# Projections of a hybrid decoder's front: three passes of rounded halves, or pairs of 64-column f32 matmuls

## The chip, the cores and the metric

The kernel runs on one core of one Trainium2 chip. The metric is device time in microseconds (us); lower is better. TensorE (PE) does the matmuls, VectorE (DVE), ScalarE (ACT) and GpSimd (POOL) the rest; SyncE's queue (SP) issues most loads.

## The reference, cut to what matters

One layer of a decoder: an input projection, three branches (dilated attention, a conformer convolution, cross-attention into 256 memory tokens), gates on their projections, an output projection, and a mixture of 32 experts of which each token takes two. 512 prompt rows and 32 sample rows go through it, all in f32.

```python
z_q, z_k, z_v, z_conv, z_mq, z_gate = split_combined(h @ lw['w_in'])
...
kv = rms_norm(mem, lw['mem_norm_g']) @ lw['w_mem_kv']
...
z = jax.nn.sigmoid(g_a) * a + jax.nn.sigmoid(g_c) * c + jax.nn.sigmoid(g_m) * m
return z @ w_out
...
for e in range(N_EXPERTS):
    hid = jax.nn.silu(h @ lw['w_expert_gate'][e]) * (h @ lw['w_expert_up'][e])
    y = y + gates[:, e:e + 1] * (hid @ lw['w_expert_down'][e])
```

## The kernel before

The front, to about 700 us, is everything ahead of the experts. Its projections go through two helpers. `mm_nat` multiplies a block of 128 rows by 256 columns of weights, with the activations stationary: the memory keys and values (`mem_kv`, 64 blocks of 128 x 128 x 256), the four heads (`project_head`, 384) and the output projection (128), 576 in all. `mm_T` keeps the weights stationary and streams half of the 544 rows (272): the gated units of the convolution (`glu`, 128 blocks), the gates (384) and the branch projections (192) of `branch`, 704 in all.

For each block both helpers issue three f32r matmuls of 128 stationary columns: high half by high half, and the two cross terms, added up in PSUM. The halves are made by `split`: ACT rounds a block of weights to f32r (`hi`, L230) and DVE subtracts it from the original (`lo`, L231). The normed rows `hTh`/`hTl`, the memory rows, the branches' inputs (`split_src`), their weights (`split_p`) and the sum ahead of the output projection (`zh`/`zl`) are kept as halves in the same way. A weight block is loaded into a slot of `ring` (six slots of 8 KB per partition, given out in turn) and its slot comes free when the halves are made; the halves stand in pool `whl` (two `hi`, two `lo`).

Between the projections PE does attention and other small work: transposes and scores of 128 columns, and matmuls of 32 columns such as `sample` (L402) and the router's logits (L1216), which put several narrow matmuls into different column ranges of the array. The experts (from 707 us) already use f32 pairs: `pg` and `pu` at L1535 (64 stationary columns, 256 streamed), `pd` at L1555 (64 and 512).

The scheduler writes each engine's order; each engine then runs its list in order and waits on semaphores. SP issues its loads in order too, so a load that waits for its slot holds back what stands behind it. Expert weights start to load when blocks come free near the end of the front.

Of the kernel before, what the change touches and what calls it, by code (L numbers as in the profile page):

```python
# [12 lines left out]
F32R = mybir.dt.float32r  # L13
# [8 lines left out]
P = 128  # L22
# [130 lines left out]
def build(tc, I, O, cols):  # L153
# [68 lines left out]
    last_lo = [None]  # L222

    def split(t, eng=(nc.vector,), pl=None):
        hi = (pl or whl).tile([P, 8, 256], F32R, name=nm("hi"), tag="w" if pl else "hi")
        lo = whl.tile([P, 8, 256], F32R, name=nm("lo"), tag="lo")
        n = 8 // len(eng)
        for q, e in enumerate(eng):
            s = slice(q * n, q * n + n)
            nc.scalar.copy(hi[:, s], v8(t)[:, s])  # L230
            last_lo[0] = e.tensor_tensor(lo[:, s], v8(t)[:, s], hi[:, s].bitcast(F32), op=ALU.subtract)  # L231
        return hi, lo
# [20 lines left out]
    hTh = hp.tile([P, 8, NT], F32R, name="hTh")  # L253
    hTl = hp.tile([P, 8, NT], F32R, name="hTl")

# [8 lines left out]
    def t_tile(name):  # L264
        return tp.tile([P, 5 * NP], F32R, name=name, tag="T")

# [11 lines left out]

    memhl = mhl.tile([P, 2, 8, NMEM], F32R, name="memhl")
    memh, meml = memhl[:, 0], memhl[:, 1]  # L280
# [3 lines left out]
    hTs = hs_.tile([P, 8, NS], F32, name="hTs", bufs=1)  # L284
# [12 lines left out]
    def loadx(src, key, at, alloc=None):  # L297
        n = src.shape[0]
        if key not in xt:
            xt[key] = alloc(nm("x")) if alloc else t_tile(nm("x")).bitcast(F32)  # L300
        v = xt[key][:, at * D:(at + 1) * D]
        last_load[0] = nc.sync.dma_start(v[:n], src)
        return v
# [33 lines left out]
    def rms_T(x, n, g, hi, lo, off, fs=None):  # L337
# [5 lines left out]
        for half in range(2):  # L343
            ps = tr.tile([P, 4, P], F32, name=nm("tr"), tag="tr")
            for kk in range(4):
                k = half * 4 + kk
                nc.tensor.transpose(ps[:, kk, :n], x[:n, k * P:(k + 1) * P], ident[:n, :n])
            c = slice(half * 4, half * 4 + 4)
            hs = hi[:, c, off:off + n]
            nc.scalar.copy(hs, ps[:, :, :n])  # L350
            nc.vector.tensor_tensor(lo[:, c, off:off + n], ps[:, :, :n], hs.bitcast(F32), op=ALU.subtract)
            if fs is not None:
                nc.scalar.copy(fs[:, c, :], ps[:, :, :n])

    for i in range(2):
        rms_T(xm[i], P, "mem_norm_g", memh, meml, i * P)
# [63 lines left out]
    def project_head(h, units, extra=()):  # L420
        T = t_tile(nm("T")).bitcast(F32).rearrange("p (s t) -> p s t", s=5)
        vh = hd.tile([P, 4, HD], F32, name=nm("vh"), tag="vh")
        vp = hd.tile([P, 4, HD], F32, name=nm("vp"), tag="vp")
        for u in range(3):
            wh, wl = split(units[u], H0ENG if h == 0 else (nc.vector,))
            for p in extra[3 + u:4 + u]:
                p.load()
            for ip in range(2):
# [3 lines left out]
                for i2 in range(2):  # L432
                    i = 2 * ip + i2
                    s = slice(i * P, (i + 1) * P)
                    mm_nat(ps[:, i2], [hTh[:, k, s] for k in range(8)], [hTl[:, k, s] for k in range(8)],
                           [wh[:, k, :] for k in range(8)], [wl[:, k, :] for k in range(8)])
# [119 lines left out]
    H0ENG = (nc.vector,) * 2  # L556
    MENG = (nc.vector, nc.vector, nc.vector, nc.gpsimd)
    def mem_kv(us_):
        al = slice(None)
        for u in us_:  # L560
            wh, wl = split(munits[u], MENG)
            ps = mm.tile([P, 2, 2, HD], F32, name=nm("mm"), tag="mm")
            for i2 in range(2):
                s = slice(i2 * P, (i2 + 1) * P)
                mm_nat(ps[:, i2], [memh[:, k, s] for k in range(8)], [meml[:, k, s] for k in range(8)],
                       [wh[:, k, :] for k in range(8)], [wl[:, k, :] for k in range(8)])
# [28 lines left out]
    class Scores:  # L595
# [3 lines left out]
        def load(self):  # L599
            h, j = self.h, self.j  # L600
            t = raw()
# [24 lines left out]
    rms_T(xs[0], P, "norm_mix_g", hTh, hTl, 0 * P)  # L626
    rms_T(xs[1], P, "norm_mix_g", hTh, hTl, 1 * P)
    mem_kv([0])
    rms_T(xs[2], P, "norm_mix_g", hTh, hTl, 2 * P)
    mem_kv([1])  # L630
    rms_T(xs[3], P, "norm_mix_g", hTh, hTl, 3 * P)
    rms_T(xs[4], NS, "norm_mix_g", hTh, hTl, NP, hTs)
# [18 lines left out]
    for h in range(4):  # L651
# [9 lines left out]
        if h == 3:  # L661
            uraw = t_tile("u").bitcast(F32)
            u = uraw[:, :4 * (30 + NP)].rearrange("p (c t) -> p c t", c=4)
            cw = uraw[:, 4 * (30 + NP):4 * (30 + NP) + 136].rearrange("p (c t) -> p c t", c=4)
            cTf = t_tile("cT").bitcast(F32)[:, :4 * NT].rearrange("p (c t) -> p c t", c=4)
# [35 lines left out]
    def mm_T(ps, wh, wl, xh, xl):  # L701
        n = len(wh)
# [5 lines left out]
    def halves(t, n):  # L708
        return [[t[:, k, f * HALF:(f + 1) * HALF] for k in range(n)] for f in range(2)]

    hH, hL = halves(hTh, 8), halves(hTl, 8)
# [30 lines left out]
    def glu(c, unit, st_tile, pl=None):  # L742
        hi, lo = split(unit, pl=pl)
        if c >= NGH:
            taps(TG[0], last_lo[0])
        half = lambda t, a: [t[:, k, a * P:(a + 1) * P] for k in range(8)]
        for f in range(2):
            pa = mm.tile([P, HALF], F32, name=nm("mm"), tag="mm")
            pb = mm.tile([P, HALF], F32, name=nm("mm"), tag="mm")
            mm_T(pb, half(hi, 1), half(lo, 1), hH[f], hL[f])  # L750
            mm_T(pa, half(hi, 0), half(lo, 0), hH[f], hL[f])
# [17 lines left out]

    for c in range(NGH):  # L770
# [4 lines left out]
    for p in pieces:  # L775
# [32 lines left out]
    def branch_loads(br, wname, j):  # L808
        gu = split(load_cols(w_in, [(GCOL + br * D + j * P, 256)]))
# [142 lines left out]
    glu(3, c3, kt_tile, ring)  # L952
# [24 lines left out]
    for f in range(NPG):  # L977
        pgs.append(mm.tile([P, HALF], F32, name=nm("mm"), tag="mm"))
        mm_T(pgs[f], *([t[:, k, :P] for k in range(8)] for t in pre[0]), hH[f], hL[f])
# [6 lines left out]
    zh, zl = [], []  # L986
    zs = zp.tile([P, 8, NS], F32, name="zs")
# [3 lines left out]
    pl_ = mst.enter_context(pool("pw", 2, side="right"))  # L991

    shs = [mg.tile([P, 4, NT], F32R, name=nm("sh"), tag="sh", bufs=2) for _ in range(2)]

    def split_src(src, lo):
        sh = shs.pop(0) if shs else mg.tile([P, 4, NT], F32R, name=nm("sh"), tag="sh", bufs=2)
        out = []
        for c in range(4):
            nc.scalar.copy(sh[:, c], src[c])
            out.append(lo(c))  # L1000
            nc.vector.tensor_tensor(out[c], src[c], sh[:, c].bitcast(F32), op=ALU.subtract)
        return halves(sh, 4), [[t[:, f * HALF:(f + 1) * HALF] for t in out] for f in range(2)]

    def am_lo(c):
        return chunks(am, "am", "lo", F32R, 1, 9)[0]

    def split_p(raw_v):
        hi = pl_.tile([P, 4, P], F32R, name=nm("ph"), tag="ph")
        lo = pl_.tile([P, 4, P], F32R, name=nm("pl"), tag="pl")
        nc.scalar.copy(hi, raw_v)  # L1010
        taps(TAPS[2], nc.vector.tensor_tensor(lo, raw_v, hi.bitcast(F32), op=ALU.subtract))
        return [hi[:, k, :] for k in range(4)], [lo[:, k, :] for k in range(4)]
# [3 lines left out]
    def branch(br, srcs, wname, first, last, then=None, hook=None):  # L1016
        sH, sL = srcs
        for j in range(8):
            if j % 2 == 0:
                (ghi, glo), npu = ahead[0] if ahead[0] is not None else branch_loads(br, wname, j)  # L1020
# [4 lines left out]
            gh, gl = ([t[:, k, (j % 2) * P:(j % 2 + 1) * P] for k in range(8)] for t in (ghi, glo))  # L1025
            ph, pl = split_p(pu[:, :, (j % 4) * P:(j % 4 + 1) * P])
            for f in range(2):
                if first and not j and f < NPG:
                    pg = pgs[f]
                else:  # L1030
                    pg = mm.tile([P, HALF], F32, name=nm("mm"), tag="mm")
                    mm_T(pg, gh, gl, hH[f], hL[f])
# [3 lines left out]
                mm_T(pp, ph, pl, sH[f], sL[f])  # L1036
                fs = slice(f * HALF, (f + 1) * HALF)
                if last and not f:
                    zh.extend(chunks(am, "am", "zh", F32R, 1, 9))
                    zl.extend(chunks(zp, "z", "zl", F32R, 1, 8) if j else chunks(am, "am", "zl", F32R, 1, 9))  # L1040
                if first:
                    nc.vector.scalar_tensor_tensor(zf[j][:, fs], th, 1.0, pp, op0=ALU.add, op1=ALU.mult)
                else:
                    nc.vector.scalar_tensor_tensor(th, th, 1.0, pp, op0=ALU.add, op1=ALU.mult)
# [39 lines left out]
    def hook(j):  # L1084
        if j in LNJ:
            conv_norm(LNJ.index(j))
        if j == LNJ[1]:
            cl = t_tile("cl")[:, :4 * NT].rearrange("p (c t) -> p c t", c=4)
            cs_.extend(split_src([cTf[:, c] for c in range(4)], lambda c: cl[:, c]))
# [25 lines left out]
    branch(0, split_src(aT, am_lo), "w_attn_proj", True, False, (2, "w_mem_proj"), attn_hook)  # L1115
    branch(2, split_src(mT, am_lo), "w_mem_proj", False, False, (1, "w_conv_proj"), hook)
# [51 lines left out]
    for k in range(8):  # L1168
        for q in range(4):
            nc.tensor.matmul(ps[32 * q:32 * q + 32], zs[:, k, :], v8(ounits[q])[:, k, :], start=(k == 0), stop=(k == 7))  # L1170
# [54 lines left out]
    for q in range(4):  # L1225
        wh, wl = split(ounits[q])
# [478 lines left out]
```

## Time and profile before

| | us |
|---|---|
| median of 3 runs | 1178.06 (1177.85 to 1178.71) |
| profiled execution | 1178.14 |
| its span | 1176.3 |
| PE busy | 1117.9 |
| DVE / ACT / POOL busy | 527.7 / 294.9 / 295.2 |
| moved by DMA | 323.86 MB, 275 GB/s on average |

A matmul's busy time holds its way through the array, so successive ones overlap; how often PE can start one is read from the distance between starts in the timeline. An f32 matmul of the program shows as two records, an f32r one and an f32 transpose as one.

### The profile page before, as it was taken

Reading aid. Unit: us, or ns where it says so; the run is one execution under the profiler, and the core shown is the slowest. Engines: PE = TensorE matmul, PEld = TensorE weight load, DVE = VectorE, ACT = ScalarE, POOL = GpSimd, SP = SyncE. Lnnn points to the kernel's source line nnn. Section 1 sums busy time; section 2 is a strip of 40 time slices with the busy share of each in tenths; the row PEclk is TensorE's granted clock in tenths of the full one; section 3 lists DMA queues with packets and bytes.
Section 4 is the critical chain, followed back from the end, with each engine's and each line's share of the span. In section 5 each row is a group of like instructions: output and inputs, shape, how many; then the busy total and the mean of one; then the engine's idle time right before and its main releaser. Section 6 shows DMA issues by size and latency. Waiting matters only on the chain. (4 is left out here: it accounts for less than half of the span.)

```text
span 1176.3 us, 21841 instructions
## 1 busy us (share of the span) xinstructions
PE 1117.9 (95%) x8965; PEld 829.6 (71%) x8965; DVE 527.7 (45%) x994; ACT 294.9 (25%) x723; POOL 295.2 (25%) x449
## 2 busy tenths in 40 slices
PE   6999999998999999999999997999999999999986
PEld 5998988886975999999998853555555555555442
DVE  6635666564884699956432264212215112122111
ACT  7434444343131522245332223000000000000000
POOL 4453545351025860222222000111111111111111
PEclk9999999998899999999999998999999999999999
DMA  9954474764676998221419179999999999999995
GB/s 322 231 155 118 134 197 118 191 186 107 233 252 234 389 368 298 73 86 58 144 65 392 73 287 363 413 413 413 413 412 410 412 410 405 405 397 405 406 406 218
DMA packets 135461, 323.86 MB, mean 275 GB/s; under 512 B 15785, under 2 KB 93105, under 8 KB 109504
## 3 DMA queue, kind: packets, MB, share of 16 engines
q1 hardware_dynamic: 125456, 310.23, 70.9%
q0 software_dynamic: 7152, 10.57, 3.8%
q10 hardware_dynamic: 2752, 1.65, 0.5%
q8 instruction: 71, 1.16, 0.4%
q14 instruction: 30, 0.25, 0.1%
HBM read 310.18 MB, written 31.49 MB: 290 GB/s over the span
## 5 line engine op out<-in xcount | busy, mean ns | idle before, releaser
L1559 POOL DMA_INDIRECT out_y_all<-work,ids x32 | 49.6, 1549 | 437.8 <-DVE work L1558 400.4
L704 PE MATMUL mm<-hTh,hi 128*128 128x272 f32 x512 | 148.5, 290 | 0.8 <-ACT hi L230 0.8
L706 PE MATMUL mm<-hTh,lo 128*128 128x272 f32 x512 | 148.5, 291 | 0.0
L705 PE MATMUL mm<-hTl,hi 128*128 128x272 f32 x512 | 147.9, 289 | 0.0
L1555 PE MATMUL pd<-w,work 128*64 128x512 f32 x512 | 118.6, 604 | 0.6 <-DVE work L1551 0.6
L1535 PE MATMUL pu<-w,xgT 128*64 128x256 f32 x992 | 113.7, 380 | 5.1 <-DMA w<-in_w_expert_up 4.3
L1535 PE MATMUL pg<-w,xgT 128*64 128x256 f32 x992 | 112.8, 379 | 1.1 <-DVE xgT L1355 0.9
L237 PE MATMUL mm<-hi,hTh 128*128 128x256 f32 x384 | 110.2, 287 | 0.0
L239 PE MATMUL mm<-hi,hTl 128*128 128x256 f32 x384 | 109.9, 286 | 0.0
L238 PE MATMUL mm<-lo,hTh 128*128 128x256 f32 x384 | 109.8, 286 | 0.0
L1545 DVE TENSOR_TENSOR work<-work,pu 128x256 f32<-128x256 f32 x32 | 19.4, 607 | 194.5 <-PE pu L1535 194.5
L1535 PEld LDWEIGHTS pg<-w,xgT 128*64 128x64 f32 x992 | 71.0, 137 | 49.8 <-issue 16.2
L1535 PEld LDWEIGHTS pu<-w,xgT 128*64 128x64 f32 x992 | 70.4, 137 | 43.8 <-DMA w<-in_w_expert_up 7.9
L704 PEld LDWEIGHTS mm<-hTh,hi 128*128 128x128 f32 x512 | 96.9, 189 | 1.7 <-ACT hi L230 1.5
L705 PEld LDWEIGHTS mm<-hTl,hi 128*128 128x128 f32 x512 | 97.0, 189 | 0.7 <-issue 0.6
L706 PEld LDWEIGHTS mm<-hTh,lo 128*128 128x128 f32 x512 | 96.2, 188 | 0.2 <-DVE lo L231 0.2
L231 DVE TENSOR_TENSOR lo<-w,hi 128x2048 fp32r<-128x2048 f32 (+2 forms) x46 | 82.2, 1804 | 30.2 <-ACT hi L230 30.2
L725 DVE SCALAR_TENSOR_TENSOR cT<-u,cT 128x512 f32<-128x512 f32 x120 | 89.1, 763 | 3.9 <-POOL cT L738 2.5
L1555 PEld LDWEIGHTS pd<-w,work 128*64 128x64 f32 x512 | 34.3, 138 | 62.5 <-issue 59.0
L1349 PE MATMUL px<-h,ohs 64*64 64x512 f16 (+1 forms) x558 | 72.5, 390 | 4.9 <-DVE gates L1431 2.9
L237 PEld LDWEIGHTS mm<-hi,hTh 128*128 128x128 f32 x384 | 72.4, 188 | 3.2 <-issue 2.8
L1543 ACT ACTIVATE work<-pg 128x256 f32<-128x256 f32 x32 | 12.3, 384 | 245.8 <-PE pg L1535 245.8
(456 smaller groups left out, 2100.1 us busy)
## 6 DMA issues: line engine op xcount, KB each, us to landing
w<-in_w_expert_gate SPq DMA_DIRECT2D x64, 1024.0 KB
w<-in_w_expert_up SPq DMA_DIRECT2D x64, 1024.0 KB
w<-in_w_expert_down SPq DMA_DIRECT2D x64, 1024.0 KB
w<-in_w_in SPq DMA_DIRECT2D x30, 512.0 KB
w<-in_w_in SPq DMA_DIRECT2D x12, 1024.0 KB
w<-in_cache_k SPq DMA_DIRECT2D x32, 256.0 KB
w<-q1d SPq DMA_DIRECT2D x16, 512.0 KB
out_k_win_sample<-in_cache_k SPq DMA_DIRECT2D x8, 1016.0 KB
```

Of the source, the lines that this page charges most:

```text
L231: last_lo[0] = e.tensor_tensor(lo[:, s], v8(t)[:, s], hi[:, s].bitcast(F32), op=ALU.subtract)
L237: nc.tensor.matmul(ps, xh[k], wh[k], start=(k == 0), stop=False)
L238: nc.tensor.matmul(ps, xh[k], wl[k], start=False, stop=False)
L239: nc.tensor.matmul(ps, xl[k], wh[k], start=False, stop=(k == n - 1))
L704: nc.tensor.matmul(ps, wh[k], xh[k], start=(k == 0), stop=False)
L705: nc.tensor.matmul(ps, wh[k], xl[k], start=False, stop=False)
L706: nc.tensor.matmul(ps, wl[k], xh[k], start=False, stop=(k == n - 1))
L725: nc.vector.scalar_tensor_tensor(cTf[:, c, :NP], u[:, c, j:j + NP], w, cTf[:, c, :NP], op0=ALU.mult, op1=ALU.add)
L1349: nc.tensor.matmul(px[CAP * f:CAP * f + CAP], oh[:64 if i == 4 else P, i, :], src[:, 4 * f:4 * f + 4, :], start=(i == GORD[0] and r == 0), ...
L1535: last = nc.tensor.matmul(ps[CAP * f:CAP * f + CAP], xT[:, k, :], ws[k // 4][:, k % 4, 256 * f:256 * f + 256], start=(k == 0), stop=(k == 7))
L1555: last = nc.tensor.matmul(pd[CAP * f:CAP * f + CAP], hT[:, kk % 2, CAP * (kk // 2):CAP * (kk // 2) + CAP], w[4 + kk // 2][:, kk % 2, 512 * ...
L1559: nc.gpsimd.indirect_dma_start(out=y2, out_offset=bass.IndirectOffsetOnAxis(ap=idc2, axis=0), in_=o, in_offset=None, bounds_check=2 * NT - ...
```

## The change

No halves are made. A block's three f32r matmuls become a pair of f32 matmuls, each with 64 of the 128 stationary columns, into the lower and the upper 64 partitions of the same PSUM tile. The weights are used where they were loaded, so a ring slot is held until the last matmul that reads it. `hT`, `memT`, the branches' inputs and `zf` are used as they are; `sample` and the small output projection read them too, in place of copies made for them. The blocks of pool `whl` now hold the key rows that `Scores` loads, which came from the ring; the first three scores of head 3 stand ahead of the convolution units. Half of the rows' transposes are copied out by DVE (`rms_T`), half by ACT. The taps of the convolution are pinned behind other marks.

```diff
-    def mm_nat(ps, xh, xl, wh, wl):
-        n = len(xh)
+    HC = P // 2
+
+    def mm_nat(ps, x, w):
+        n = len(x)
         for k in range(n):
-            nc.tensor.matmul(ps, xh[k], wh[k], start=(k == 0), stop=False)
-            nc.tensor.matmul(ps, xh[k], wl[k], start=False, stop=False)
-            nc.tensor.matmul(ps, xl[k], wh[k], start=False, stop=(k == n - 1))
+            for g in range(2):
+                c = slice(HC * g, HC * g + HC)
+                nc.tensor.matmul(ps[c], x[k][:, c], w[k], start=(k == 0), stop=(k == n - 1))
...
-            nc.tensor.matmul(ps, wh[k], xh[k], start=(k == 0), stop=False)
-            nc.tensor.matmul(ps, wh[k], xl[k], start=False, stop=False)
-            nc.tensor.matmul(ps, wl[k], xh[k], start=False, stop=(k == n - 1))
+            for g in range(2):
+                c = slice(HC * g, HC * g + HC)
+                nc.tensor.matmul(ps[c], w[k][:, c], x[k], start=(k == 0), stop=(k == n - 1))
...
-            wh, wl = split(units[u], H0ENG if h == 0 else (nc.vector,))
+            w = v8(units[u])
...
-            t = raw()
+            t = wslot(("hi", "lo")[j % 2])
...
-        gu = split(load_cols(w_in, [(GCOL + br * D + j * P, 256)]))
+        gu = v8(load_cols(w_in, [(GCOL + br * D + j * P, 256)]))
...
-            ph, pl = split_p(pu[:, :, (j % 4) * P:(j % 4 + 1) * P])
+            ph = [pu[:, k, (j % 4) * P:(j % 4 + 1) * P] for k in range(4)]
+            taps(TAPS[2], zmark[0])
...
-                    if last:
-                        nc.scalar.copy(zh[j][:, fs], zf[j][:, fs])
-                        if f:
-                            nc.gpsimd.tensor_copy(zs[:, j], zf[j][:, NP:])
-                        nc.vector.tensor_tensor(zl[j][:, fs], zf[j][:, fs], zh[j][:, fs].bitcast(F32), op=ALU.subtract)
...
-        wh, wl = split(ounits[q])
+        w = v8(ounits[q])
```

PE's order in a head's projection, where an attention piece of the head before (`tr`, from `vh` and `vp`) stands between the matmuls of one PSUM tile. Before:

```order
L239 MATMUL mm_1582<-hi_1569,hTl 128x256
L237 MATMUL mm_1582<-hi_1569,hTh 128x256
L238 MATMUL mm_1582<-lo_1570,hTh 128x256
L519 MATMUL tr_1252<-vh_630,PT_1249 128x128 x2
L522 MATMUL tr_1252<-vp_631,PT_1249 32x128 x4
L239 MATMUL mm_1582<-hi_1569,hTl 128x256
L237 MATMUL mm_1582<-hi_1569,hTh 128x256
L238 MATMUL mm_1582<-lo_1570,hTh 128x256
```

With the change (a matmul to 64 partitions is one half of a pair):

```order
L228 MATMUL mm_1175<-w_897,hT 64x256 x16
L504 MATMUL tr_979<-vh_508,PT_976 128x128 x2
L507 MATMUL tr_979<-vp_509,PT_976 32x128 x4
L228 MATMUL mm_1175<-w_897,hT 64x256
L228 MATMUL mm_1236<-w_897,hT 64x256 x15
L511 MATMUL tr_987<-ident,PT_976 128x128
L497 MATMUL tr_1009<-ident,P_991 128x128 x2
L498 MATMUL tr_1009<-ident,P_991 96x128
L228 MATMUL mm_1236<-w_897,hT 64x256 x17
```

The piece stood inside a group of three; it now stands between halves of a pair, which leaves a lone half in front and behind.

SP's order at the second and third weight unit of head 0 (`w_204`, `w_207` before), with what each load waits for. Before:

```order
L637 DMA gsm<-in_mq_norm_g 32x128 [waits DMAHW0_49]
L638 DMA gsm<-in_mq_norm_g 32x128 [waits DMAHW1_49]
L639 DMA gsm<-in_q_norm_g 32x128 [waits DMAHW2_49]
L218 DMA w_204<-in_w_in 128x8x128 [waits DMAHW3_49,DVE_49,Pool_49]
L218 DMA w_204<-in_w_in 128x8x128 [waits DMAHW4_49]
...
L218 DMA w_207<-in_w_in 128x8x128 [waits DMAHW1_49,DVE_49,Pool_49]
```

With the change (`w_198`, `w_201`; `ws` are the key rows of the scores):

```order
L587 DMA ws_914<-in_cache_k 128x4x128 [waits DMAHW4_49]
L663 DMA wr<-in_w_router_group 128x8x4 [waits DMAHW5_49]
L665 DMA wr<-in_w_router_expert 128x8x8 [waits DMAHW6_49]
L217 DMA w_198<-in_w_in 128x8x128 [waits DMAHW7_49,PE_49]
L217 DMA w_198<-in_w_in 128x8x128 [waits DMAHW0_49]
...
L217 DMA w_201<-in_w_in 128x8x128 [waits DMAHW1_49,PE_49]
```

The units waited for the subtractions on DVE and POOL that freed their slots; they now wait for the matmuls, and six loads of key rows have moved ahead of them.

## Rows read from the trace of the kernel before

**Rows 1.** The page, part 1: busy time of each engine over the span.
```profile
PE 1117.9 (95%) x8965; PEld 829.6 (71%) x8965; DVE 527.7 (45%) x994; ACT 294.9 (25%) x723; POOL 295.2 (25%) x449
```

**Rows 2.** Windows: width, then busy us (records) of PE, PEld, DVE, ACT, POOL; PEclk, DMA.
```profile
26.00:722.00 696.00, 675.28 (x5627) 592.68 (x5627) 413.48 (x778) 247.90 (x627) 233.59 (x397) 0.98 0.60 194
550.00:600.00 50.00, 50.00 (x401) 50.00 (x400) 22.09 (x35) 18.21 (x32) 13.60 (x18) 1.00 0.24 85
722.00:1090.00 368.00, 357.61 (x2732) 188.28 (x2730) 85.48 (x176) 25.22 (x52) 40.32 (x26) 1.00 1.02 409
1090.00:1176.00 86.00, 69.17 (x502) 33.60 (x498) 13.23 (x22) 4.26 (x9) 9.25 (x6) 0.97 0.87 343
```

**Rows 3.** Windows of line L704, then of L237: busy us (records) of PE and PEld.
```profile
0.00:722.00 722.00, 203.90 (x704) 132.95 (x704) 0.98 0.61 199
0.00:722.00 722.00, 165.41 (x576) 109.06 (x576) 0.98 0.61 199
```

**Rows 4.** Timeline of PE, a branch (272 streamed columns): start us, us, instruction.
```profile
447.34 0.29 PE L704 MATMUL mm<-hTh,hi 128*128 128x272 f32 x1
447.46 0.28 PE L705 MATMUL mm<-hTl,hi 128*128 128x272 f32 x1
447.58 0.29 PE L706 MATMUL mm<-hTh,lo 128*128 128x272 f32 x1
447.71 0.29 PE L704 MATMUL mm<-hTh,hi 128*128 128x272 f32 x1
...
451.85 0.29 PE L704 MATMUL mm<-hTh,hi 128*128 128x272 f32 x1
```

**Rows 5.** Timeline of PE, a head's projection (256 streamed columns).
```profile
151.45 0.28 PE L237 MATMUL mm<-hi,hTh 128*128 128x256 f32 x1
...
152.88 0.28 PE L237 MATMUL mm<-hi,hTh 128*128 128x256 f32 x1
```

**Rows 6.** Timeline of PE, one expert.
```profile
1001.34 0.44 PE L1549 MATMUL ph<-ident,work 128*128 128x128 f32 x2
1002.14 0.66 PE L1354 MATMUL px<-ident,xgT 128*128 128x128 f32 x4 [0.36 <-ACT xgT L1351]
1002.73 3.65 PE L1555 MATMUL pd<-w,work 128*64 128x512 f32 x16
1006.21 3.62 PE L1535 MATMUL pg<-w,xgT 128*64 128x256 f32 x32
1009.66 3.62 PE L1535 MATMUL pu<-w,xgT 128*64 128x256 f32 x32
1013.22 0.40 PE L1349 MATMUL px<-h,ohs 64*64 64x512 f16 x2
```

**Rows 7.** Timeline of PE, transposes between f32r matmuls, then `sample` cut by transposes.
```profile
139.72 1.03 PE L453 MATMUL tr<-ident,A 128*128 128x128 f32 x8
140.51 0.36 PE L237 MATMUL mm<-hi,hTh 128*128 128x256 f32 x1
140.71 0.28 PE L238 MATMUL mm<-lo,hTh 128*128 128x256 f32 x1
...
143.00 3.65 PE L402 MATMUL mm<-w,hTs 128*32 128x256 f32 x46
146.57 0.66 PE L453 MATMUL tr<-ident,A 128*128 128x128 f32 x4
147.16 0.62 PE L402 MATMUL mm<-w,hTs 128*32 128x256 f32 x2
147.71 0.39 PE L237 MATMUL mm<-hi,hTh 128*128 128x256 f32 x1
```

**Rows 8.** Timeline of PE, the router's logits between f32r matmuls.
```profile
654.37 0.28 PE L237 MATMUL mm<-hi,zh 128*128 128x256 f32 x1
654.58 0.62 PE L1216 MATMUL pl<-h2T,wr 128*32 128x256 f32 x4
655.12 0.39 PE L238 MATMUL mm<-lo,zh 128*128 128x256 f32 x1
655.35 0.28 PE L239 MATMUL mm<-hi,zl 128*128 128x256 f32 x1
```

**Rows 9.** Waits of PE, 26 to 722 us: us in total, times, longest.
```profile
PE mm L238 <- DVE lo L231: 1.5, 2, 0.9
PE mm L704 <- ACT hi L230: 0.8, 1, 0.8
```

**Rows 10.** The chain that ended last: start us, us, what.
```profile
1168.20 0.45 POOLq L1637
```

**Rows 11.** Waits of SP, 612 to 760 us.
```profile
SPq L587 <- PE mm L239: 26.3, 1, 26.3
```

More of the change, by code (lines that the diff above doesn't have):

```diff
@@ L299, in loadx @@
         if key not in xt:
-            xt[key] = alloc(nm("x")) if alloc else t_tile(nm("x")).bitcast(F32)
+            xt[key] = alloc(nm("x")) if alloc else t_tile(nm("x"))
         v = xt[key][:, at * D:(at + 1) * D]
@@ L336, in build, with rms_T @@
     VENG = nc.scalar
-    def rms_T(x, n, g, hi, lo, off, fs=None):
+    def rms_T(x, n, g, dst, off):
         sq = npl.tile([P, D], BF16, name=nm("xn"), tag="xn", bufs=1)
@@ L348, in rms_T @@
             c = slice(half * 4, half * 4 + 4)
[L349 to L353, printed above, removed]
+            if half:
+                nc.vector.tensor_copy(dst[:, c, off:off + n], ps[:, :, :n])
+            else:
+                nc.scalar.copy(dst[:, c, off:off + n], ps[:, :, :n])
     for i in range(2):
-        rms_T(xm[i], P, "mem_norm_g", memh, meml, i * P)
+        rms_T(xm[i], P, "mem_norm_g", memT, i * P)
     pt = tr.tile([P, 8], F32, name=nm("tr"), tag="tr")
@@ L434, in project_head @@
                     s = slice(i * P, (i + 1) * P)
-                    mm_nat(ps[:, i2], [hTh[:, k, s] for k in range(8)], [hTl[:, k, s] for k in range(8)],
-                           [wh[:, k, :] for k in range(8)], [wl[:, k, :] for k in range(8)])
+                    mm_nat(ps[:, i2], [hT[:, k, s] for k in range(8)], [w[:, k, :] for k in range(8)])
                 A = hs_.tile([P, 2, 2, HD], F32, name=nm("A"), tag="A", bufs=3)
@@ L564, in mem_kv @@
                 s = slice(i2 * P, (i2 + 1) * P)
-                mm_nat(ps[:, i2], [memh[:, k, s] for k in range(8)], [meml[:, k, s] for k in range(8)],
-                       [wh[:, k, :] for k in range(8)], [wl[:, k, :] for k in range(8)])
+                mm_nat(ps[:, i2], [memT[:, k, s] for k in range(8)], [w[:, k, :] for k in range(8)])
             h0 = 2 * (u % 2)
@@ L740, in build, with glu @@
     glu_end = [None]
-    def glu(c, unit, st_tile, pl=None):
-        hi, lo = split(unit, pl=pl)
+    def glu(c, unit, st_tile):
+        w = v8(unit)
         if c >= NGH:
-            taps(TG[0], last_lo[0])
+            taps(TG[0], marks[-1])
         half = lambda t, a: [t[:, k, a * P:(a + 1) * P] for k in range(8)]
@@ L749, in glu @@
             pb = mm.tile([P, HALF], F32, name=nm("mm"), tag="mm")
[L750 to L751 removed]
+            mm_T(pb, half(w, 1), hH[f])
+            mm_T(pa, half(w, 0), hH[f])
             th = st_tile()[:, :HALF]
@@ L768, in near_load @@
         return t
+    for p in pieces[:3]:
+        p.score(last_att[0])
     for c in range(NGH):
@@ L774, in build @@
             p.load()
-    for p in pieces:
+    for p in pieces[3:]:
         p.score(last_att[0])
@@ L951, in build @@
         mem_scores(bp)
-    glu(3, c3, kt_tile, ring)
+    glu(3, c3, kt_tile)
     glus[0] += 1
@@ L978, in build @@
         pgs.append(mm.tile([P, HALF], F32, name=nm("mm"), tag="mm"))
-        mm_T(pgs[f], *([t[:, k, :P] for k in range(8)] for t in pre[0]), hH[f], hL[f])
+        mm_T(pgs[f], [pre[0][:, k, :P] for k in range(8)], hH[f])
     smp.close()
@@ L990, in build @@
     mm2 = mst.enter_context(pool("mm2", 3, PSUM))
[L991 to L1012, printed above, removed]
+    zmark = [glu_end[0]]
     ahead = [pre]
     def branch(br, srcs, wname, first, last, then=None, hook=None):
-        sH, sL = srcs
+        sH = halves(srcs)
         for j in range(8):
             if j % 2 == 0:
-                (ghi, glo), npu = ahead[0] if ahead[0] is not None else branch_loads(br, wname, j)
+                gw, npu = ahead[0] if ahead[0] is not None else branch_loads(br, wname, j)
                 ahead[0] = None
@@ L1087, in hook @@
         if j == LNJ[1]:
-            cl = t_tile("cl")[:, :4 * NT].rearrange("p (c t) -> p c t", c=4)
-            cs_.extend(split_src([cTf[:, c] for c in range(4)], lambda c: cl[:, c]))
+            cs_.extend(cTf[:, c] for c in range(4))
     def conv_out():
@@ L1169, in build @@
         for q in range(4):
-            nc.tensor.matmul(ps[32 * q:32 * q + 32], zs[:, k, :], v8(ounits[q])[:, k, :], start=(k == 0), stop=(k == 7))
+            nc.tensor.matmul(ps[32 * q:32 * q + 32], zf[k][:, NP:], v8(ounits[q])[:, k, :], start=(k == 0), stop=(k == 7))
     nc.vector.scalar_tensor_tensor(x1s, ps, 0.5, x1s, op0=ALU.mult, op1=ALU.add)
@@ L1230, in build @@
                 s = slice((2 * ip + i2) * P, (2 * ip + i2 + 1) * P)
-                mm_nat(ps[:, i2], [zh[k][:, s] for k in range(8)], [zl[k][:, s] for k in range(8)],
-                       [wh[:, k, :] for k in range(8)], [wl[:, k, :] for k in range(8)])
+                mm_nat(ps[:, i2], [zf[k][:, s] for k in range(8)], [w[:, k, :] for k in range(8)])
             for g in ([slice(0, 2)] if not SPL[q][ip] else [slice(0, 1), slice(1, 2)]):
```

70 lines of the change are left out of this document (25 added, 45 removed).

## The prediction

> **What bounds the kernel now.** I read the page's busy times first, then the windows by stage, then PE's timeline for the distance between starts. PE is busy 95% of the span, the other engines under half [rows 1]. From 26 us to the end of the first expert at 722 us it is busy 675.3 of 696 us [rows 2], so only 20.7 us of that stretch can be waiting. In a stretch of branches it is busy all 50 of 50 us [rows 2]. Then come the experts: to 1090 us PE is busy 357.6 of 368 us while DMA runs at 409 GB/s, and only in the last 86 us is it idle for longer, 16.8 us [rows 2], of which about 8 us lie behind the last release at 1168.2 [rows 10]. So the front is a queue of PE work, and the reader is to see that what counts is how much time the new matmuls take on PE, not what DVE and ACT are spared.
>
> **The old price.** A branch block starts a new triple every (451.85 − 447.34)/12 = 0.376 us [rows 4]; the window agrees, 50 us / 401 records = 0.125 us for one [rows 2]. A head's block takes (152.88 − 151.45)/4 = 0.357 us [rows 5]. There are 704 blocks of the first kind and 576 of the second [rows 3]: 704 × 0.376 + 576 × 0.357 = 264.7 + 205.6 = 470.3 us.
>
> **The new price.** The same form runs in the experts: 64 stationary columns, 256 streamed, f32, alternating between the lower and the upper half of the output. Its 32 records for `pg` take 1009.66 − 1006.21 = 3.45 us [rows 6]. A matmul is two records and a pair four, so eight pairs take 3.45 us, 0.431 us a pair; the two halves do run together there, since one record's own 0.38 us is far more than the 0.108 us between starts. For 512 streamed columns four pairs take 1006.21 − 1002.73 = 3.48 us, 0.870 us a pair [rows 6]. Between the two a streamed column adds 0.439/256 = 0.00171 us, so 272 columns take 0.431 + 16 × 0.00171 = 0.459 us. The new blocks differ in one thing: both halves stream the same block and hold different columns, where the experts' halves hold the same and stream different weights. The router's logits do the former: two narrow stationary blocks for one streamed one, four records in 0.54 us [rows 8], two steps of 0.22 and a change of width. I see no reason for another price. Sum: 576 × 0.431 + 704 × 0.459 = 248.3 + 323.1 = 571.4 us, that is **+101.1 us**. PE's clock is granted at full 2.4 GHz in both stretches (1.00) [rows 2], so nothing is to be scaled.
>
> A rule on passes bears on this. The rows give two records a matmul, each 0.216 us for 256 columns. The Trainium skill, FP8 and Floating Point Precision, TensorE Precision Notes, says that true FP32 makes four passes through the array. With each pass at the f32r price of these rows, four would cost 4 × 0.119 = 0.476 us and 4 × 0.125 = 0.501 us, +156 us in place of +101; the trace shows a cheaper pair, and the sum goes by it.
>
> **Lone halves.** The scheduler puts attention pieces between matmuls, and in the new order 79 of the runs end on an odd number of halves so far, as the first place shown in the change does. A lone narrow matmul costs its full two steps: the last one of `sample`, cut off by transposes, takes 147.71 − 147.16 = 0.55 us [rows 7], 0.43 and a change of width. If each cut pair leaves two lone halves, that is 79 × 0.431 = 34 us. But after the cut the next run begins with the upper half of one step and goes on with the lower half of the next, other columns of the array, which can run beside it; then only the 24 runs with an odd count lose a step of 0.22, **+5 us**. I take 5: of its 46 records, `sample` packs three column ranges as they come, 3.57 us or about 16 steps of 0.22 [rows 7], with no regard to which belong to one step. 34 is the upper end.
>
> **Changes of width.** Three f32r matmuls have the full 128 columns, as the transposes do; eight transposes between them take 0.79 us, 0.10 each, and the triple behind them is late by 0.08 [rows 7]: going there is almost free. Pairs are narrow. Leaving them costs 0.11 (`pu` takes 3.56, `pg` 3.45) and four transposes ahead of a narrow matmul take 0.59 where four at 0.10 take 0.40 [rows 6]: together 0.30 us a visit. Visits to 32-column work pay this already: 0.09, 0.11 and 0.11 us around the logits [rows 8]. The new order has 97 visits, 63 of them wide at both ends, the old one 120, 41 with a narrow end. New: 97 × 0.30 = 29 us; old: 22 narrow at both ends × 0.31 and 19 at one × 0.16 = 10 us. The difference is 19; some first matmuls are late anyway for other reasons, so I take **+15 us**, bounds 5 and 29.
>
> The Trainium skill, TensorEngine Tiling (Array Packing), Key Properties, says that changing the tiling mode drains the engine; that is the direction of these rows, and it gives no price.
>
> **What goes.** DVE and ACT lose the halves, but they are off the path: PE waited 1.5 us for `lo` and 0.8 us for `hi` in the whole front [rows 9]. The other 18 us of its idle time [rows 2] are chains of small steps in attention and routing that stay; fuller queues on DVE and ACT can have lengthened some of them. I take **−8 us**, bounds 0 and 20.7.
>
> **What is moved.** Ring slots are held until the matmuls have read them, and SP's loads of head 0's second and third unit wait for PE with six loads of key rows ahead, as shown in the change. Behind them stand the units of the next heads. Between a slot's release and its use lies at least one other unit's work, 32 pairs or 14 us, while a 1 MB block at the 409 GB/s of [rows 2] needs 2.6 us: cost nothing, as long as SP isn't held for over 10 us; without that cover each unit costs its 2.6 us, for the 12 head units 31 us. The scores' loads in `whl` wait for scores of a head before, which DVE does early. In the output projection four ring slots free later than before, but the expert loads behind them waited for its end anyway, 26.3 us in one wait [rows 11]. The experts' part is not touched and follows PE's start, so their 454 us move as a block: 0, bounds −8.7 (the idle time of the last stretch beyond the end, if the loads get ahead) and +3.
>
> **Sum** against the profiled execution's own 1178.14 us, which is its span of 1176.3 and 1.8 around it, and 0.1 above the median: 1178.1 + 101.1 + 5 + 15 − 8 = 1291; I put **1290 us**, own range 1274 to 1306.
>
> **Rivals.**
> 1. *Cut pairs leave lone halves.* For it: the order's 79 cuts, and the 0.55 us of a lone matmul. Against: `sample`'s packing. 1290 + 29 = 1319 us.
> 2. *Loads become late.* SP is held by a wait of a score, and units arrive late; 31 us as above, 1321 us. Against: the releases lie a unit ahead.
> 3. *The front had slack.* All 20.7 us of PE's idle time and the 8.7 us of the tail go, and visits cost no more than 5: 1178 + 101 + 5 + 5 − 29 = 1260 us. For it: DVE and ACT have less to do. Against: almost none of that idle time is put down to the halves [rows 9].
> 4. *Four records at the old price.* If the two halves, because they share the streamed block, went through the array one record after another at the f32r pace: 1178 + 156 + 12 = 1346 us. Against: the overlap in [rows 6, 8]. It is where the four passes of the Trainium skill, FP8 and Floating Point Precision, TensorE Precision Notes, would lead.
> 5. *Faster.* A pair that reads one streamed block costs only one of the two steps, 0.216 us: then the front loses 470 − 286 = 184 us, 994 us. The kernel gets faster when a pair costs under 470/1280 = 0.367 us on average. Against: the logits, which share the streamed block too, take two steps [rows 8]; nothing speaks for it.
>
> **Chances.** Forecast 72%, rival 1 8%, rival 2 6%, rival 3 8%, rival 4 4%, rival 5 2%. The forecast's own range holds some six or seven in ten; the range for eight reaches to rival 3 below and rival 1 above, 1258 to 1320. A change of under 0.2% (2.4 us), about what a measurement of this kernel can't tell from none, would need a pair to cost what a triple does; 1%. Faster 2%, slower 97%.
>
> **What would show it.** In the profile after, the 32 records of eight pairs should take 3.67 us in a branch and 3.45 in a head; behind a cut the halves should go on two at a time from the first step (rival 1: 0.43 us of a lone half on both sides); PE near 100% busy from 30 to 800 us; DVE's and ACT's busy time down by more than 80 us each with no gain; experts at 14 us each, starting some 110 us later. I am wrong if a pair in the branches takes other than 0.459 us, or if PE shows waits for loads in the heads.

## The result, and the profile after

The changed kernel takes **1292.01 us** (median of 4 runs, 1289.55 to 1292.27) against 1177.95 (1172.51 to 1178.71) for the kernel before on the same chip: ratio 1.0975, 95% interval 1.0939 to 1.101. It is slower by 114 us. The profiled execution's span is 1290.3 us, 114.0 more than the 1176.3 of before.

Part 1 of the page of the changed kernel, which answers to [rows 1], and two groups of its part 5, the pairs:

```profile
PE 1234.9 (96%) x10244; PEld 712.9 (55%) x10245; DVE 414.8 (32%) x888; ACT 201.0 (16%) x611; POOL 240.4 (19%) x437
...
L688 PE MATMUL mm<-hT,w 128*64 128x272 f32 x1920 | 249.1, 393 | 0.0
...
L228 PE MATMUL mm<-w,hT 128*64 128x256 f32 x1536 | 178.8, 382 | 0.0
```

DVE is busy 113 us less, ACT 94 us less, and PE 117 us more. To see where the 114 us lie I cut both traces at the same places of the program, not at the same times: at the first projection matmul of head 0, behind the last head's last one, at the transposes of `u` with which the attention to the cached tokens is over, at the router's first `pr`, and at the first `pg` of expert 0. Windows of the kernel before (busy time of PE alone, then PEclk, DMA), cut so:

```profile
0.00:42.80 42.80, 31.13 (x237) 1.00 0.96 287
42.80:255.40 212.60, 210.02 (x1912) 1.00 0.61 165
255.40:384.50 129.10, 120.48 (x1002) 0.93 0.60 203
384.50:620.80 236.30, 235.40 (x1869) 0.99 0.53 187
620.80:700.10 79.30, 77.10 (x607) 0.98 0.67 259
```

Windows of the changed kernel at the same five places:

```profile
0.00:49.50 49.50, 40.05 (x319) 1.00 0.93 279
49.50:302.40 252.90, 252.90 (x2310) 1.00 0.54 145
302.40:442.50 140.10, 128.68 (x1098) 0.95 0.53 174
442.50:722.60 280.10, 280.10 (x2414) 1.00 0.42 146
722.60:813.80 91.20, 89.00 (x769) 1.00 0.62 240
```

The five stages are longer by 6.7, 40.3, 11.0, 43.8 and 11.9 us, together 113.7. (Ahead of that `pr` the kernel before had already done 10 blocks of the output projection, 3.7 us. Counted with the last stage, they make the branches longer by 47.5 us, where 576 blocks at 0.459 − 0.376 us are 47.8.) From the first `pg` to the end it is 476.2 us before and 476.5 after, so the experts only moved. PE's idle time in the five stages falls from 26.0 us (700.1 − 674.13) to 23.1 (813.8 − 790.72): the heads (2.6 us) and the branches (0.9) lost all of theirs, the stage between them has 11.4 in place of 8.6. The front was PE's queue and still is. In a second execution of the changed kernel (`after_twin`, below), cut at its own places, the idle time is 19.0 us: the same but for the third stage, which has 7.4.

The price of a pair is the predicted one. Timeline of PE in a branch of the changed kernel (what answers to [rows 4]; two outputs interleave):

```profile
500.06 3.82 PE L688 MATMUL mm<-hT,w 128*64 128x272 f32 x30
...
505.56 3.82 PE L688 MATMUL mm<-hT,w 128*64 128x272 f32 x30
```

Between these two rows lie 48 records of one kind, 12 pairs, in 5.50 us: 0.458 us a pair, forecast 0.459. In the heads (what answers to [rows 5, 7]):

```profile
84.60 0.66 PE L438 MATMUL tr<-ident,A 128*128 128x128 f32 x4
85.19 6.70 PE L228 MATMUL mm<-w,hT 128*64 128x256 f32 x60
91.81 0.66 PE L438 MATMUL tr<-ident,A 128*128 128x128 f32 x4
...
97.99 0.65 PE L228 MATMUL mm<-w,hT 128*64 128x256 f32 x2
98.57 0.33 PE L459 MATMUL tr<-ident,A 128*128 128x128 f32 x1
...
144.66 3.67 PE L228 MATMUL mm<-w,hT 128*64 128x256 f32 x32
148.26 1.13 PE L537 MATMUL tr<-PT,mv 128*128 128x256 f32 x4
```

60 records, 15 pairs, take 91.81 − 85.19 = 6.62 us: 15 × 0.431 is 6.47, and 0.15 goes on leaving for the full-width transposes. Ahead of the run four transposes take 0.59, as in [rows 6]. A half that stands alone (98.57 − 97.99) takes 0.58: two steps of 0.216 and the 0.15. The 32 records at 144.66 begin with an upper half, because a transpose cut the pair in two; they take 3.60 us, the same 8 × 0.431 + 0.15 as a run that begins with a lower half.

One wait had no term of its own. Timelines of PE and then of DVE in the changed kernel, where the near keys are transposed:

```profile
375.53 0.27 PE L845 MATMUL psA<-ident,S 128*128 128x128 f32 x1
380.28 1.08 PE L833 MATMUL tr<-ident,w 128*128 128x128 f32 x4 [4.48 <-issue]
```
```profile
371.93 7.83 DVE L707 SCALAR_TENSOR_TENSOR cT<-u,cT 128x512 f32<-128x512 f32 x10
379.68 0.40 DVE L742 SCALAR_TENSOR_TENSOR u<-st,mm 128x240 f32<-128x240 f32 x1
380.00 0.18 DVE L744 SCALAR_TENSOR_TENSOR us<-st,mm 128x32 f32<-128x32 f32 x1
```

The profile puts PE's 4.48 us down to nothing ("issue"). But every second block of these transposes writes to a tile of `mm`, which the last GLU block had, and DVE's two last readers of it (L742, L744) end at 380.08 and 380.18, behind ten taps of the convolution. The next transposes start 0.1 us after the second.

### The profile page after: what moved, and what is told of

The parts are those of the page before. It is cut to its first block, busy times and chain, and to the rows that moved or that the text cites. A ratio compares the mean times of both kernels' runs of the same rounds, so it can differ in the third digit from the quotient of the medians.

```text
span 1290.3 us, 24098 instructions
## 1 busy us (share of the span) xinstructions
PE 1234.9 (96%) x10244; PEld 712.9 (55%) x10245; DVE 414.8 (32%) x888; ACT 201.0 (16%) x611; POOL 240.4 (19%) x437
## 5 line engine op out<-in xcount | busy, mean ns | idle before, releaser
L688 PE MATMUL mm<-hT,w 128*64 128x272 f32 x1920 | 249.1, 393 | 0.0
L688 PEld LDWEIGHTS mm<-hT,w 128*64 128x64 f32 x1920 | 148.1, 137 | 83.3 <-issue 2.6
L228 PE MATMUL mm<-w,hT 128*64 128x256 f32 x1536 | 178.8, 382 | 0.0
L228 PEld LDWEIGHTS mm<-w,hT 128*64 128x64 f32 x1536 | 107.3, 137 | 58.8 <-issue 9.1
L1005 POOL TENSOR_TENSOR z<-z,gth 128x272 f32<-128x272 f32 x32 | 26.3, 823 | 222.1 <-DVE gth L1004 222.1
L228 PE MATMUL mm<-w,z 128*64 128x256 f32 x512 | 59.6, 382 | 0.1
L1511 DVE TENSOR_SCALAR work<-pd,gates 128x512 f32<-128x512 f32 x32 | 24.0, 751 | 93.6 <-PE pd L1508 93.6
L1302 PEld LDWEIGHTS <-ohs 64*64 64x64 f16 (+1 forms) x558 | 28.9, 109 | 42.9 <-issue 20.8
L997 ACT ACTIVATE gth<-mm 128x272 f32<-128x272 f32 x48 | 19.0, 396 | 213.6 <-PE mm L688 213.5
L228 PEld LDWEIGHTS mm<-w,z 128*64 128x64 f32 x512 | 35.9, 137 | 20.8 <-issue 4.3
```

The costliest lines, as they stand in the source:

```text
L228: nc.tensor.matmul(ps[c], x[k][:, c], w[k], start=(k == 0), stop=(k == n - 1))
L688: nc.tensor.matmul(ps[c], w[k][:, c], x[k], start=(k == 0), stop=(k == n - 1))
L997: nc.scalar.activation(th, pg, AF.Tanh, scale=0.5)
L1302: nc.tensor.matmul(px[CAP * f:CAP * f + CAP], oh[:64 if i == 4 else P, i, :], src[:, 4 * f:4 * f + 4, :], start=(i == GORD[0] and r == 0), ...
L1511: nc.vector.tensor_scalar(o, pd, gc, None, op0=ALU.mult)
```

## The experiments

All are compared with runs of the kernel before on the same chip: 1176.65 us median for `full_width`, `g_outer`, `two_passes` and `f16_halves`; 1177.28 for `full_width_timed`, `after_twin`, `taps_later` and `halves_back`; 1179.19 for `halves_apart` and `halves_free`.

**One matmul of 128 columns for each pair** (`full_width`). From the changed kernel, the same products:

```diff
-            for g in range(2):
-                c = slice(HC * g, HC * g + HC)
-                nc.tensor.matmul(ps[c], w[k][:, c], x[k], start=(k == 0), stop=(k == n - 1))
+            nc.tensor.matmul(ps, w[k], x[k], start=(k == 0), stop=(k == n - 1))
```

and likewise in `mm_nat`.

> From the changed kernel, each pair becomes one f32 matmul of all 128 stationary columns (same sum, same two records, no narrow matmul). Theory, that only the streamed columns count: two records at 0.216 us for 256 columns as in the pair, so the price stays 0.431, and the changes of width (15 us) and odd halves (5 us) go: about 1272 us. Rival, that the load of 128 f32 columns no longer hides behind the streaming, as in the attention scores of before, where two records of 128 x 256 took 0.63 us (149.79 to 150.42): 0.2 us more a block, 1280 blocks, about 1530 us.

1270.15 us (one run). The same kernel, timed six times (`full_width_timed`):

> The kernel with one f32 matmul of 128 stationary columns in place of each pair, timed against the kernel before in rounds. Theory (lone halves and changes of width together cost some 20 us of the changed kernel's time, and the 64 columns buy nothing): 1268 to 1272 us. Rival (the one run of it was a chance value): nearer to 1290 us.

**1271.17 us** (1268.95 to 1273.83, 6 runs), ratio 1.0799, 95% interval 1.0768 to 1.0829. Timeline of PE of this kernel, a head, then a branch:

```profile
82.46 7.07 PE L226 MATMUL mm<-w,hT 128*128 128x256 f32 x32
89.37 0.60 PE L436 MATMUL tr<-ident,A 128*128 128x128 f32 x4
89.81 0.38 PE L226 MATMUL mm<-w,hT 128*128 128x256 f32 x1
```
```profile
479.50 3.83 PE L684 MATMUL mm<-hT,w 128*128 128x272 f32 x16
483.17 2.00 PE L684 MATMUL mm<-aT,w 128*128 128x272 f32 x8
```

A full-width matmul is two records, 6.91/32 = 0.216 and 3.67/16 = 0.229 us each: 0.432 and 0.459 a step, a pair's price. So two halves of 64 columns run beside each other exactly as far as one matmul of 128 would, and halving the columns buys nothing. There is no 0.15 on leaving, and the four transposes take 0.44 where pairs follow them at 0.59. The rival (1530 us) is out. What the form with pairs costs beyond the price of its steps is 1290.1 − 1271.2 = 19 us (1290.1 is `after_twin`, on the same chip).

**All lower halves first, then all upper** (`g_outer`). From the changed kernel, in both helpers:

```diff
-        for k in range(n):
-            for g in range(2):
-                c = slice(HC * g, HC * g + HC)
+        for g in range(2):
+            c = slice(HC * g, HC * g + HC)
+            for k in range(n):
```

> From the changed kernel, the same matmuls in another order: all lower halves of a PSUM tile, then all upper halves. Theory, that the price of 0.431 us rests on two halves next to each other in PE's order that run together: every half alone takes 0.431 us, so 1280 blocks cost 571 us more, less 0.4 us at each of some 160 tiles where the last lower and the first upper half meet: 1790 to 1865 us. Rival, that PE pulls later halves ahead by itself: about 1292 us.

1567.27 us (one run), between the two. Timeline of PE of this kernel, then of the changed kernel:

```profile
551.49 10.47 PE L688 MATMUL mm<-hT,ws 128*64 128x272 f32 x56
561.89 0.28 PE L943 MATMUL tr<-ident,PB 128*32 128x128 f32 x1
```
```profile
359.65 14.15 PE L688 MATMUL mm<-hT,w 128*64 128x272 f32 x122
373.73 1.97 PE L833 MATMUL tr<-ident,w 128*128 128x128 f32 x16
```

10.40/56 = 0.186 us a record, where the changed kernel has 14.08/122 = 0.115 and records with nothing beside them would have 0.229. Single records of this stretch show why it is between. In the program eight matmuls of one half, 16 records, stand ahead of eight of the other. Of such a row 8 records run alone, 0.229 apart; around each change of half the last 4 of the one run beside the first 4 of the other. So a row takes 12 steps, 2.81 us and not 3.67. The overlap needs the other half close behind in the queue. The theory had it that only direct neighbours overlap, and that is too narrow: about two matmuls of the other half are taken ahead.

**Two of the three passes** (`two_passes`). From the kernel before, one cross term of each triple left out, so that the product with the activations' low half is missing. In `mm_nat`, shown here, that is the third matmul; in `mm_T` it is the second (`wh[k]`, `xl[k]`):

```diff
-            nc.tensor.matmul(ps, xh[k], wl[k], start=False, stop=False)
-            nc.tensor.matmul(ps, xl[k], wh[k], start=False, stop=(k == n - 1))
+            nc.tensor.matmul(ps, xh[k], wl[k], start=False, stop=(k == n - 1))
```

> From the kernel before, the second cross term (third f32r matmul of each block) is left out; the halves are made as before. Theory, that the front is a queue of PE work at 0.119 and 0.125 us a matmul: 576 x 0.119 + 704 x 0.125 = 157 us less, about 1021 us, perhaps some us more where waits for halves begin to show. Rival, that making the halves on ACT and DVE is nearly as long as PE's work and becomes the bound: less than half of it, above 1100 us.

1092.77 us (one run): 84 us less in place of the 157 of a queue with nothing else in it. Windows of this kernel, all engines as in [rows 2], and PE's longest waits:

```profile
26.00:300.00 274.00, 249.87 (x2177) 210.27 (x2176) 183.17 (x364) 121.42 (x399) 125.12 (x206) 0.93 0.70 193
400.00:520.00 120.00, 93.31 (x662) 88.79 (x661) 100.72 (x145) 47.87 (x79) 27.45 (x26) 0.90 0.44 149
```
```profile
PE mm L1063 <- DVE cT L723: 16.9, 2, 16.2
PE mm L703 <- ACT ph L1008: 8.0, 1, 8.0
```

Below the old price the front is not PE's alone: PE idles 24 us of the 274 and 27 of the 120 and its granted clock falls to 0.93 and 0.90, where the kernel before idles 11 and none in the same stretches of time (which hold somewhat other work). The longest waits are for the convolution's taps (`cT`) and for ACT's high halves of the branches' weights (`ph`). Making PE's work longer cost all of it, as in the change; shortening it gave about half back, by this one run. So the theory is refuted, and the time is a little below the rival's 1100. The rival's reason is borne out only in part, since the longest wait is for taps and not for halves.

**Halves as f16** (`f16_halves`). From the kernel before, `hi` and `lo` as f16 in place of f32r, in all triples:

```diff
-        hi = (pl or whl).tile([P, 8, 256], F32R, name=nm("hi"), tag="w" if pl else "hi")
-        lo = whl.tile([P, 8, 256], F32R, name=nm("lo"), tag="lo")
+        hi = f16v((pl or whl).tile([P, 2048], F32, name=nm("hi"), tag="w" if pl else "hi"))
+        lo = f16v(whl.tile([P, 2048], F32, name=nm("lo"), tag="lo"))
```

> From the kernel before, the halves are f16 in place of f32r, three matmuls as before (f16 times f16 into f32). Theory, that an f32r matmul of 256 columns takes 0.119 us where the streaming alone is 0.109 (a bf16 matmul of 128 x 256 in the router starts every 0.109 us) and the rest is the load of its f32 weights: 1728 x 0.010 + 2112 x 0.009 = 36 us less than before, about 1142 us. Rival, that the pace has nothing to do with the type: 1178 us. Second rival, that f16 outputs cost ACT and DVE more and PE waits for halves: above 1185 us.

**1137.96 us** (1136.33 to 1140.73, 4 runs), ratio 0.9685, 95% interval 0.9648 to 0.9722: faster than both kernels. Timeline of PE of this kernel, a branch:

```profile
420.53 0.28 PE L707 MATMUL mm<-hTh,hi 128*128 128x272 f16 x1
...
420.88 0.28 PE L707 MATMUL mm<-hTh,hi 128*128 128x272 f16 x1
```

A triple takes 0.35 us where [rows 4] have 0.376; in the heads the starts are 0.109 apart, where [rows 5] have 0.119. Three passes at these prices come to some 37 us less than before, as measured (38.7). The runs show the shorter distance between starts; that the load of f32 weights is its cause, as the theory says, they do not show.

**The changed kernel again** (`after_twin`), to compare the runs that follow with. The last two ran on another chip; there the comparison goes by the ratios to the kernel before.

> The changed kernel once more, unaltered, on the same chip as the kernels beside it, so that they are compared with it and not only with the kernel before. Both theories: 1290 to 1293 us.

1290.09 us (1289.26 to 1292.29, 6 runs), ratio 1.0966, 95% interval 1.0936 to 1.0996.

**The taps behind the last GLU block** (`taps_later`). From the changed kernel:

```diff
     for mark in marks[:8]:
-        taps(TAPS[0], marks[-1])
+        taps(TAPS[0], glu_end[0])
```

> The changed kernel, with the first ten convolution taps put behind the last GLU block of the first branch in place of behind an attention mark, so that DVE releases GLU's output tiles before the taps. Theory (the 4.5 us wait of the four transposes at 380 us is the price of these taps standing ahead of the releases): the wait goes and the time falls by 4 to 5 us, to about 1287.5 us. Rival (PE's place is lost anyway, or the taps hold something else up later): within 1.5 us of the changed kernel.

1285.63 us (1284.5 to 1292.22, 6 runs), ratio 1.0933, 95% interval 1.0899 to 1.0966: 4.5 us below the changed kernel by the medians, though the ranges overlap. Timeline of PE of this kernel at the same place, and the window that answers to the third of the changed kernel's five:

```profile
373.38 1.97 PE L833 MATMUL tr<-ident,w 128*128 128x128 f32 x16
375.29 1.04 PE L833 MATMUL tr<-ident,w 128*128 128x128 f32 x8
376.27 1.04 PE L833 MATMUL tr<-ident,w 128*128 128x128 f32 x8
```
```profile
303.30:435.90 132.60, 124.22 (x1098) 1.00 0.54 177
```

The wait is gone. The stage takes 132.6 us, with the granted clock at 1.00. In the first execution of the changed kernel it took 140.1 at 0.95, with the 4.48 us of wait. The execution of `after_twin` shows the same place otherwise, timeline and window:

```profile
381.43 0.63 PE L833 MATMUL tr<-ident,w 128*128 128x128 f32 x4 [0.62 <-issue]
```
```profile
302.10:440.30 138.20, 130.83 (x1097) 0.94 0.51 168
```

Here PE ran at half clock from 330.5 to 347.6 us and came 5 us later to the transposes (378.74 in place of 373.73). The wait is only 0.62 us, but PE goes on at the same release: DVE's last reader ends at 381.32, behind the same ten taps. So the taps are the cause of the wait in both executions. How much of the 5.6 to 7.5 us of the stage is the wait's price and how much the clock's is not settled: the clock also fell in `after_twin` ahead of the wait, and not in this run.

**The halves' work put back without a reader** (`halves_back`). To the changed kernel, for each weight unit of heads, memory, GLU and gates, a copy and a subtraction of which nothing is used:

```diff
+    def spare_split(t):
+        nc.scalar.copy(scr_hi, t)
+        nc.vector.tensor_tensor(scr_lo, t, scr_hi, op=ALU.subtract)
+        return t
...
-            w = v8(units[u])
+            w = spare_split(v8(units[u]))
```

> The changed kernel, with the making of rounded halves put back as work without a reader: of each weight unit of heads, memory, GLU and gates one ACT copy and one DVE subtraction of 128 x 2048 into spare tiles, which is most of what the change took off these two engines. Theory (the relief of DVE and ACT was worth little, 8 us at most): 0 to 8 us above the changed kernel, 1292 to 1300. Rival 3 of the prediction (the front had slack that the relief sets free, some 29 us in all): 20 us or more above it, 1312 and up.

1323.57 us (1322.48 to 1326.14, 6 runs), ratio 1.1249, 95% interval 1.1218 to 1.1279: 33.5 us above the changed kernel. My theory's 0 to 8 is refuted for this kernel. The loss lies ahead of the end of the last head: the window of its heads, and DVE's longest wait in it:

```profile
58.60:337.50 278.90, 264.88 (x2308) 159.62 (x2307) 123.19 (x246) 90.79 (x309) 93.04 (x161) 0.96 0.47 127
```
```profile
DVE scr_lo L249 <- ACT scr_hi L248: 63.0, 13, 11.4
```

The start is 9.1 us longer, the heads 26.0 (PE idle 14.0 us of them, and a lower granted clock), and what follows up to the first `pg` is 3.6 us shorter. DVE stood 63 us for ACT's copies. PE's longest waits there were 6.2 us for POOL's `A` and 5.3 for ACT's `aT`, small steps of attention. Two kernels were to tell whether the load, the wait of one engine for the other, or the time itself was the cause.

**The same, each engine on its own** (`halves_apart`): `tensor_tensor(scr_lo, t, t, ...)`, so that only the load is waited for.

> As the run that put the halves back, reading the weight units again, but the subtraction does not wait for ACT's copy: both only wait for the load. Theory (the load is what holds the engines, 63 us of DVE's time in the heads): still 20 us or more above the changed kernel, 1310 us and up, DVE's wait now put down to the load. Rival (the wait of DVE for ACT and of ACT for DVE over the single spare tiles is what cost): 1290 to 1300 us.

1320.09 us (1315.96 to 1323.0, 6 runs), ratio 1.1197, 95% interval 1.1165 to 1.1229: by the ratios 27 us above the changed kernel. DVE's longest wait of this kernel, 26 to 340 us, is now put down to the load:

```profile
DVE scr_lo L249 <- DMA w<-in_w_in: 56.0, 14, 11.0
```

So the two engines' wait for each other is not the main cause.

**The same work on a resident tile** (`halves_free`): both operations read the normalised tokens (or the memory's) in place of the unit.

> The changed kernel with the same spare copies on ACT and subtractions on DVE, of the same size, number and place in the program as in the run before, but reading a resident tile (the normalised tokens, or the memory's) in place of the weight unit, and the subtraction reads no result of ACT. So the two engines carry the work without waiting for a load or for each other. Theory (work on DVE and ACT is worth little by itself; the 33 us of the run before are DVE and ACT held for a unit that is not there yet, with attention's small steps queued behind): 0 to 8 us above the changed kernel, 1290 to 1298 us. Rival (it is the time on these engines that counts, so the change gained some 30 us by the relief): 1310 us and up.

1306.69 us (1306.1 to 1308.62, 6 runs), ratio 1.1089, 95% interval 1.1062 to 1.1116: 16.6 us above the changed kernel by the medians and 14.5 by the ratios, between theory and rival: both missed. So about half of the loss is waiting for units that aren't there yet, and the other half comes from the work itself. The window of this kernel's heads, and DVE's spare operations from 40 to 330 us:

```profile
48.50:320.30 271.80, 259.17 (x2318) 161.56 (x2315) 148.33 (x258) 105.77 (x320) 110.90 (x161) 0.98 0.51 136
```
```profile
L252 DVE TENSOR_TENSOR scr_lo<-hT 128x2048 f32<-128x2048 f32 x27 | 62.0, 2297 | 0.5
```

The heads are 18.9 us longer than the changed kernel's, PE idle 12.6 us of them, and the next stage 2.6 us shorter. With nothing to wait for, the schedule drew 27 of the 32 spare operations into this stretch, where the kernel before had made 14 to 17 lower halves. PE's waits there are for attention's small steps: 8.8 us for POOL's `A` (L385) and 3.4 for DVE's (L375). So the work on DVE and ACT is not free: put there in bulk, it delays these steps. Which of the two engines counts more was not tried, since both got their work back together. How much of this the kernel before paid is not settled by these runs; its own heads show 2.6 us of idle PE.

## Why the prediction was right

The forecast of 1290 us was right within 2 us, by the mechanism that it names; two of its smaller terms, of opposite sign, were both too large, and their errors nearly cancel. By its steps, against a difference of 114.0 us in span (111.9 in the execution of `after_twin`):

- **What bounds the kernel.** Right: the stages of heads and branches are 100% busy on PE after the change, and the 207 us that DVE and ACT were spared bought 2.9 us of idle time, 7.0 in `after_twin`.
- **Price of the pairs, +101.1.** Right: 0.458 and 0.431 us a pair against 0.376 and 0.357 a triple. A sum over all records, from start to next start, gives 591.9 us for pairs and 490.7 for triples, +101.2, but that it equals the price is luck: beyond the price the pairs hold 5.0 us of lone halves and 14.9 on leaving, the triples some 17 us at changes of width, 2.4 of waits and 1.2 of lower clock. That halves which share the streamed block would cost the same as the experts' halves is shown by these rows, and `full_width` shows that the array would do the same with 128 columns at once.
- **Lone halves, +5.** Right: of the 98 runs of pairs 24 are odd, each 0.21 us longer than an even run beyond its records' price, 5.0 us. Cut pairs do go on two at a time (the row at 144.66), so **rival 1** is out.
- **Changes of width, +15.** The mechanism is right, the size somewhat high. Every run costs 0.15 us on leaving, and four transposes ahead of a run take 0.59 in place of 0.44: the 0.30 a visit. The Trainium skill, TensorEngine Tiling (Array Packing), Key Properties, has a drain there without a price, and these rows agree. What is left for this term is 114.0 − 101.1 − 5.0 + 2.9 − 0.3 (the experts) = 10.5 us, and 12.5 by the numbers of `after_twin`: a remainder, with stretches at a lower granted clock in both kernels in it. A count explains its size. The new order pays 98 × 0.30 = 29 us, as forecast. For the old one the prediction had 10 us, because it called the 0.08 us behind transposes [rows 7] almost free. In the trace of before, 70 such first matmuls are late by 7.8 us together, which makes the old changes 17 us. `full_width`, without pairs, is 19 us faster, 5.0 of them lone halves; the other 14 are its saving in changes of width and the rest.
- **What goes, −8.** 2.9 us in the first execution, the step that was sized worst there, and 7.0 in `after_twin`. The idle time of the heads did go, 2.6 us, and 2.2 of the start's, in both. In the first the stage behind the heads took 2.8 back, with the wait of 4.5 us for a tile behind ten taps; in `after_twin` that wait was 0.62 us and the stage at lower clock. The prediction had DVE's and ACT's fuller queues as the reason of idle time, and did not ask what a shifted order puts in front of a release on DVE. `taps_later` shows the removal of that wait. **Rival 3**, that all slack goes, is out: 23.1 of 26.0 us stayed, or 19.0. The reason given for the small term (these engines are off the path) fits the waits of the kernel before [rows 9]; as a rule it is refuted by `halves_free`, where such work in bulk costs some 15 us.
- **Moved loads, 0.** Right: PE shows no wait at all in the heads, and the first to the last expert take the same time. The prediction's condition, that SP is not held for over 10 us, did not hold: SP stood up to 28.1 us in one wait there (for DVE's `den`, L526), and the units still came in time. **Rival 2** is out. The chain that ended last, which answers to [rows 10], shows the tail unmoved:

```profile
1281.94 0.45 POOLq L1590
```

  from there 8.4 us to the end, 8.1 before.
- **Rival 4** (four records at the old price) and **rival 5** (one step a pair) needed 0.50 and 0.22 us a pair; 0.458 and 0.431 put both out. The Trainium skill, FP8 and Floating Point Precision, TensorE Precision Notes, counts four passes for true FP32, without a price for one. These rows agree if a pass costs what a matmul of `f16_halves` does: 4 × 0.116 = 0.46 us for 272 columns and 4 × 0.109 = 0.44 for 256, where `full_width` takes 0.459 and 0.432. What the prediction had wrong there was the f32r price for a pass (4 × 0.125), which its sum did not use.

Two errors nearly cancel: 4.5 us too much for width and 5.1 too much for what goes in the first execution, 2.5 and 1.0 in `after_twin`. The price of the pairs carries the forecast; that the total came within 2 us is in part luck.

## What to carry to other kernels

Before trading passes for another form of matmul, find the new form somewhere in the trace and take the distance between starts, not one record's own time: here 0.431 us a step against 0.357 decided everything. Narrow stationary blocks bought nothing here, where all 128 columns were there: one full-width matmul costs the same and saves the lone halves and the changes of width (19 us). Three passes of f16 halves, at 0.33 and 0.35 us a block, were faster than both forms compared here. And work taken off engines that are not the bound returned only a part of the idle time that the bounding engine had, while a shifted order can put new work ahead of a release.

## What was not expected of the hardware

None of this is in the prediction; the first and the third were forecast ahead of their own runs.

- An f32 matmul with 128 stationary columns costs what two of 64 cost side by side: 0.432 us for 256 streamed columns, 0.459 for 272.
- Halves of the array overlap over more than direct neighbours: 4 of 16 records at each change of half in `g_outer`.
- f16 triples start every 0.116 us for 272 columns where f32r triples start every 0.125 [rows 4], both of 128 stationary columns and at the same granted clock.
